# Spreading four pieces of token sums over two merges and the row blocks between them

## The chip, the cores and the metric

The kernel runs on one core of one Trainium2 chip. The metric is the time of one execution in device microseconds (us), and less is better. A core has five engines that run side by side, each with an instruction queue of its own that it works off in order: PE (matrix multiply, TensorE), ACT (ScalarE), DVE (VectorE), POOL (GpSimd) and SP (SyncE, which here only starts DMA transfers). An engine that waits for a semaphore holds everything that stands behind that instruction in its queue. On-chip data lie in SBUF, results of matmuls in PSUM; the DMA engines move data between these and the device's main memory (HBM).

## What is computed

The reference is one transformer-like block on 2048 tokens of width 1024, in float32. Cut to what matters here:

```python
merged = gate_a * (y_attn @ w_branch_attn) + gate_b * (y_gmlp @ w_branch_gmlp)
y = merged @ w_out
x = x + rmsnorm(y, norm_post_mix)
h = rmsnorm(x, norm_pre_mlp)
a = relu(h @ w_mlp_in)
x = x + rmsnorm((a * a) @ w_mlp_out, norm_post_mlp)
```

The parts before (input projections, dilated attention, chunked gMLP) are done when the stages of this document begin. The gates are sigmoids of stored projections.

## The kernel before

Tokens are worked in four chunks of 512, in the order 2, 3, 0, 1 (list `chunks`, line 986). This text calls them first to fourth chunk by that order, so the third is `c == 0` and the fourth `c == 1`. For each chunk there are two stages.

**Merge** (`merge`, line 885): eight slices `dt` of 128 output channels. For each slice PE makes the two branch products into PSUM (18 matmuls, names `b`, `yt`, `wb`). Two gates come from memory (`load_gate`, line 870, an SP transfer, line 873) into buffers `g` of which there are three for one branch and two for the other; ACT applies the sigmoid (`open_gate`, line 882); DVE multiplies gate and product (line 899) and adds the two (line 901); then `split` (ACT at line 70, DVE at line 78) makes a high and a low part of the result, called `mg`. Every matmul of this kernel is three matmuls of such parts (`mm3`, lines 95 to 97). The gates of a slice are asked for one slice ahead; those of the first two slices of the next chunk, and the next `yt`, are loaded after the first row block of this chunk.

**Row blocks** (`out_block`, line 912): four blocks of 128 tokens. SP loads the residual rows (`xr`, line 917, one buffer); PE multiplies `mg` with `w_out` (name `o`, 48 matmuls); ACT squares and sums (line 936), DVE scales (937), the residual is added (DVE, line 941), ACT sums its squares (943), POOL starts the store of `x1d` (944), and DVE writes the normed rows `y` (946). A second part of the block, run later by `flush` or `flush_older`, has PE transpose `y` (line 951, name `pt`), ACT copies it into `tt` (952), POOL starts two stores to `h2d` (953). `flush_older` runs in the middle of a later row block, when two blocks are open, and `flush` behind slices 0 and 2 of the next merge.

**Token sums** (`sums_t`, line 966). The MLP's first matmul is done by a scheme with fewer products, which needs sums and differences of quarters of `h2d`. For each half of the tokens there are four pieces, `k` from 0 to 3. A piece loads four tiles of 128 x 512 from `h2d` (SP, line 974), makes four subtractions on POOL (lines 975 to 978) and starts four stores to `t_d` on POOL (line 980). Two of the four tiles lie in one buffer `tq` (one copy, `bufs=1`), the other two in `tr` (two copies); both belong to the pool `ttp`, which the fourth chunk's second row block gives back (`e2r.close()`). The trace shows all of them under the name `tq`, the stores under `td`. The sums of the half stored first (chunks 2 and 3) are made by `merge_sums` (line 982) in the third merge, one piece behind each of the slices 4, 5, 6 and 7. They are read as `T_first` at the start of the MLP, behind the fourth chunk.

**Order of the work.** The order on PE is that of the program. On the other engines a planner orders the instructions by the program's order and its estimate of when each can run, so an instruction may stand earlier than written. `behind()` (line 170) limits that: what is emitted inside it stands, on each of ACT, DVE, POOL and SP, behind the instruction that was emitted last on that engine. The sums of the other half, later in the kernel, use it already (lines 1346 to 1348).

```python
    def merge_sums(dt):
        if dt > 3:
            sums_t(1, dt - 4, ttp, "tq", "tr", 2)
```

Of the kernel before, what the change touches and what calls it, by code (L numbers as in the profile page):

```python
# [41 lines left out]
def block_kernel(ctx, tc, a, out):  # L42
# [4 lines left out]
    def stack(es, name, bufs=1, side=None, space=None):  # L47
        kw = dict(name=name, bufs=bufs, reuse_waits="tile")
        if side:
            kw["side"] = side  # L50
        if space is not None:
            kw["space"] = space
        return es.enter_context(tc.tile_pool(**kw))
# [7 lines left out]
    def psum_mm(name):  # L61
        return ps.tile([P, 512], F32, name=name, tag="mm")
# [4 lines left out]
    def split(hi, lo, src, hi_eng="act", lo_eng="dve"):  # L67

        if hi_eng == "act":
            act.activation(hi, src, AF.Copy)  # L70
        elif hi_eng == "pool":
            pool.tensor_scalar(hi, src, 1.0, 1.0, op0=OP.mult, op1=OP.mult)  # L72
        else:
            dve.tensor_copy(hi, src)
        if behind_product is not None and lo_eng == "dve":
            behind_product.append((lo, src, f32(hi)))
        else:
            (pool if lo_eng == "pool" else dve).tensor_sub(lo, src, f32(hi))  # L78
# [15 lines left out]
    def mm3(ps, lh, ll, rh, rl, start, stop):  # L94
        pe.matmul(ps, lh, rh, start=start, stop=False)  # L95
        pe.matmul(ps, lh, rl, start=False, stop=False)  # L96
        pe.matmul(ps, ll, rh, start=False, stop=stop)  # L97
# [72 lines left out]
    def behind():  # L170

        es, t = ExitStack(), mybir.EngineType
        for e in (t.Activation, t.DVE, t.Pool, t.SP):
            es.enter_context(tc.issue_after(next(i for i in reversed(nc.cur_bb.bb.instructions) if i.engine == e)))
        return es
# [594 lines left out]
    for n in range(len(units) + 1):  # L770
        u = None
        if n < len(units):
            g, c, j = units[n]
# [73 lines left out]
    def load_y(c, engs=("act", "dve")):  # L847
        cs = slice(c * 512, (c + 1) * 512)
        yt = [bot.tile([P, 2, 512], F32R, name=f"yt{c}{k}", tag=f"yt{k}") for k in range(6)]
        for k in range(6):  # L850
            split_in(yt[k], ya_d[k, :, cs] if k < 2 else yg_d[k - 2, :, cs], None, *engs)
        return yt
# [17 lines left out]
    def load_gate(c, dt, wch):  # L870
        if (c, dt, wch) not in gates:
            gt = gtp.tile([P, 512], F32, name=f"g{wch}_{c}{dt}", tag=f"gt{wch}", bufs=3 - wch)
            sp.dma_start(gt, gate_d[wch * 8 + dt, :, c * 512:(c + 1) * 512])
            gates[c, dt, wch] = gt
# [3 lines left out]
    def open_gate(c, dt, wch):  # L878
        if (c, dt, wch) not in opened:
            load_gate(c, dt, wch)  # L880
            gt = gates[c, dt, wch]
            act.activation(gt, gt, AF.Sigmoid)
            opened.add((c, dt, wch))

    def merge(c, yt, between, each=None):
        cs = slice(c * 512, (c + 1) * 512)
        mg = []
        for dt in range(KT):
            dsl = slice(dt * P, (dt + 1) * P)
            if dt % 4 == 0:  # L890
                mg.append(mgp[dt // 4].tile([P, 2, 4, 512], F32R, name=f"mg{c}{dt}", tag="mg"))
            parts = []
            for wch, ks in ((0, range(0, 2)), (1, range(2, 6))):
                open_gate(c, dt, wch)
                gt = gates.pop((c, dt, wch))
                p = psum_mm(f"b{wch}_{c}{dt}")
                for k in ks:
                    mm3(p, wb[k][:, 0, dsl], wb[k][:, 1, dsl], yt[k][:, 0, :], yt[k][:, 1, :], k == ks[0], k == ks[-1])
                dve.tensor_mul(gt, gt, p)
                parts.append(gt)  # L900
            dve.tensor_add(parts[0], parts[0], parts[1])
            split(mg[-1][:, 0, dt % 4, :], mg[-1][:, 1, dt % 4, :], parts[0])
            if dt < KT - 1:
                for wch in range(2):
                    open_gate(c, dt + 1, wch)
            if each:
                each(dt)
            if dt in between:
                between[dt]()
        return mg  # L910
# [55 lines left out]
    def sums_t(half, k, pl, tag, tag2, bufs2):  # L966

        w = pl.tile([P, 2, 512], F32, name=f"tq{half}{k}", tag=tag, bufs=1)
        b11, b12 = w[:, 0], w[:, 1]
        b21, b22 = ((wp3 if pl is not ttp else pl).tile([P, 512], F32, name=f"tq{half}{k}{n}", tag=tag2, bufs=bufs2)  # L970
                    for n in range(2))
        t0 = half * HALF
        for t, kk, c in ((b11, k, 0), (b12, k, 1), (b22, k + 4, 1), (b21, k + 4, 0)):
            sp.dma_start(t, h2_d[:, kk, t0 + c * 512:t0 + c * 512 + 512])
        pool.tensor_sub(b11, b12, b11)
        pool.tensor_sub(b12, b22, b12)
        pool.tensor_sub(b22, b22, b11)
        pool.tensor_sub(b21, b21, b22)
        for name, t in (("T1", b11), ("T3", b12), ("T2", b22), ("T4", b21)):
            pool.dma_start(t_d[half][:, T_AT.index(name), k], t)  # L980

    def merge_sums(dt):
        if dt > 3:
            sums_t(1, dt - 4, ttp, "tq", "tr", 2)

    chunks = (2, 3, 0, 1)
    FIRST = ((0, 0), (1, 0), (0, 1), (2, 0), (1, 1))
# [14 lines left out]
    def load_b(half, name):  # L1002

        w = r3.tile([P, 2, 4, 512], F32R, name=f"{name}_{half}", tag=name, bufs=1)
        for k in range(0, 4, 2):
            t0, k0 = half * HALF, k + (4 if name == "B21" else 0)
            split_in(w[:, :, k:k + 2], h2_d[:, k0:k0 + 2, t0:t0 + 512], None, "act")
        b_[half, name] = w
# [39 lines left out]
    def lone_a(half, q, n, raw=None):  # L1048
        raw_lone(half, q, n, raw)
        split_lone(half, q, n)  # L1050
# [147 lines left out]
    ttp = None  # L1198
    yt = load_y(2, ("pool", "pool"))
    early_gates(2)  # L1200
    mg = merge(2, yt, {}, spatial_out)
    for n, c in enumerate(chunks):
        if n:
            mg = merge(c, yt, {0: flush, 2: flush}, merge_sums if c == 0 else None)
        for i in range(4):
            b = out_block(c, i, mg, flush_older)
            next(b)
            last.append(b)
            if n < 3 and not i:
                yt = load_y(chunks[n + 1])  # L1210
                for dt in range(2):
                    for wch in range(2):
                        load_gate(chunks[n + 1], dt, wch)
            if n == 3 and i == 1:
                e2r.close()
                rx = stack(e3, "rx", 1, side="right")
                spare = rx.tile([P, 512], F32, name="ar1_4", tag="xs", bufs=LEAD + 1)
                r3 = stack(er, "r3", 1, side="right")
                for name in ("B11", "B21"):
                    load_b(1, name)  # L1220
                for o, (q, n_) in enumerate(FIRST):
                    raw = gtp.tile([P, 512], F32, name=f"ar{n_}_{q}", tag=f"gt{o % 2}", bufs=3 - o % 2)
                    lone_a(1, q, n_, raw.rearrange("p (k c) -> p k c", k=4))
# [111 lines left out]
    tq = stack(eq, "tq", 1)  # L1335
# [440 lines left out]
```

## Time and profile before

| what | value |
|---|---|
| median of 3 runs | 2699.76 us (2698.89 to 2700.78) |
| the profiled execution | 2700.86 us |
| its span | 2698.8 us |
| mean granted clock of PE | 0.996 of full speed |
| busy share PE, DVE, ACT, POOL | 99%, 59%, 39%, 36% |
| packets of SP's DMA queue q1 | 43.5% of 16 engines' span |

The span is the time from the first to the last instruction that the profiler recorded on the core; the profiled execution's time also holds what lies around it, 2.06 us. A line of the timeline reads: start, duration, engine, line of the code, operation, output `<-` inputs by the program's names, count, and in brackets the idle time of the engine just before it with what ended that idle time. SPq, PEld and the like are the engine's queue or its weight loads. A table by windows gives, for each stretch of time, the busy time of every engine in it and the clock that was granted to PE.

### The profile page before, as it was taken

To read this page: it belongs to the slowest core of one execution; us is meant where nothing else is said; L and a number is where in the kernel's file an instruction comes from. 1 tells how busy PE (TensorE), PEld (TensorE's weight loads), DVE (VectorE), ACT (ScalarE), POOL (GpSimd) and SP (SyncE) were. 2 spreads that over 40 slices of the span, in tenths; PEclk is the share of its full clock that TensorE was granted. 3 is DMA by queue.
4 is the path that set the end of the run, shared out by engine and by line. 5 is a ranking of instruction groups with operands and counts; after the bars stand their busy time and mean duration, and the time that the engine had idled before them with its cause. 6 is when DMAs were issued, how large, how long until landed. Compare 5 with 4: busy or idle time off the path is not lost. (4 is left out here: it accounts for less than half of the span.)

```text
span 2698.8 us, 34839 instructions
## 1 busy us (share of the span) xinstructions
PE 2663.4 (99%) x12674; PEld 2226.9 (83%) x12674; DVE 1582.5 (59%) x2677; ACT 1053.2 (39%) x2149; POOL 977.2 (36%) x837
## 2 busy tenths in 40 slices
PE   9999999999999999999899999999999999999998
PEld 8888888888888888888678888888888888888887
DVE  5665463334444345665456765555437888888866
ACT  5213111144444432344335555565545333333334
POOL 0351352210050004210413454323224776676645
PEclk9999999999999999999999999999999999999999
DMA  7445446266577846654656465554344212222236
GB/s 271 167 144 180 152 141 218 96 189 199 177 248 205 220 151 187 202 177 145 227 172 251 133 207 178 173 183 125 114 136 129 84 57 86 88 86 87 92 108 212
DMA packets 299197, 431.77 MB, mean 160 GB/s; under 512 B 52817, under 2 KB 166225, under 8 KB 299026
## 3 DMA queue, kind: packets, MB, share of 16 engines
q1 hardware_dynamic: 226864, 370.48, 43.5%
q10 hardware_dynamic: 64178, 32.06, 3.9%
q0 software_dynamic: 7984, 27.01, 2.6%
q8 instruction: 100, 1.64, 0.3%
q14 instruction: 71, 0.58, 0.1%
HBM read 286.67 MB, written 142.80 MB: 159 GB/s over the span
## 5 line engine op out<-in xcount | busy, mean ns | idle before, releaser
L1627 PE MATMUL ya<-T_spots,s 128*128 128x512 f32 x1176 | 289.4, 390 | 0.7 <-ACT T_spots L70 0.6
L1627 PEld LDWEIGHTS ya<-T_spots,s 128*128 128x128 f32 x1176 | 220.6, 188 | 47.4 <-ACT T_spots L70 1.0
L70 ACT ACTIVATE s<-sraw 128x768 fp32r<-128x768 f32 (+1 forms) x184 | 127.2, 696 | 330.4 <-POOL sraw L1428 155.7
L78 DVE TENSOR_TENSOR s<-sraw,s 128x512 fp32r<-128x512 f32 x172 | 184.1, 1095 | 8.6 <-ACT s L70 8.5
L1104 PE MATMUL aa<-B,A 128*128 128x512 f32 x768 | 182.3, 390 | 0.7 <-DVE A L85 0.7
L1104 PEld LDWEIGHTS aa<-B,A 128*128 128x128 f32 x768 | 143.9, 188 | 31.2 <-DVE A L85 1.1
L1627 PE MATMUL yc<-T_spots,s 128*128 128x512 f32 x624 | 159.7, 389 | 0.0
L72 POOL TENSOR_SCALAR w_g<-w_g_r 128x1024 fp32r<-128x1024 f32 x32 | 34.1, 1080 | 344.5 <-PE g L97 258.0
L1075 POOL TENSOR_TENSOR s<-w1r 128x512 f32<-128x512 f32 x32 | 42.3, 1322 | 309.3 <-DVE S L78 256.6
L95 PE MATMUL x<-hT_a,wq 128*128 128x512 f32 x384 | 149.8, 390 | 0.0
L96 PE MATMUL x<-hT_a,wq 128*128 128x512 f32 x384 | 149.5, 389 | 0.0
L97 PE MATMUL x<-hT_a,wq 128*128 128x512 f32 x384 | 149.5, 389 | 0.0
L709 DVE TENSOR_REDUCE o<-po 128x256 f32<-128x512 f32 x48 | 33.1, 690 | 184.3 <-PE po L708 184.3
L1627 PEld LDWEIGHTS yc<-T_spots,s 128*128 128x128 f32 x624 | 117.2, 188 | 24.3
L70 ACT ACTIVATE hl<-r 128x512 fp32r<-128x512 f32 x48 | 30.4, 632 | 238.1 <-POOL r L307 89.0
L95 PE MATMUL o<-wo,mg 128*128 128x512 f32 x256 | 102.1, 399 | 8.1 <-ACT mg L70 7.5
L78 POOL TENSOR_TENSOR T_spots<-w2r,T_spots 128x512 fp32r<-128x512 f32 x70 | 104.5, 1522 | 7.3 <-ACT T_spots L70 7.3
L95 PE MATMUL g<-hT_b,w_g 128*128 128x512 f32 x256 | 104.7, 409 | 0.0
L95 PE MATMUL g<-hT_a,w_g 128*128 128x512 f32 x256 | 104.3, 407 | 0.0
L78 DVE TENSOR_TENSOR A<-w1r,A 128x512 fp32r<-128x512 f32 x61 | 61.8, 1014 | 66.9 <-ACT A L70 66.9
L96 PE MATMUL o<-wo,mg 128*128 128x512 f32 x256 | 101.0, 394 | 0.0
L97 PE MATMUL o<-wo,mg 128*128 128x512 f32 x256 | 100.9, 394 | 0.0
(390 smaller groups left out, 7156.2 us busy)
## 6 DMA issues: line engine op xcount, KB each, us to landing
w1r<-in_w_mlp_in_dram SPq DMA_DIRECT2D x64, 512.0 KB, 3.8
sraw<-sd SPq DMA_DIRECT2D x128, 256.0 KB, 3.3
qk<-hl SPq DMA_DIRECT2D x24, 1024.0 KB, 5.1
qq<-qk SPq DMA_DIRECT2D x96, 256.0 KB, 4.9
w_g_r<-in_w_in_dram SPq DMA_DIRECT2D x32, 512.0 KB, 5.5
gated<-gt SPq DMA_DIRECT2D x64, 256.0 KB, 3.5
w2r<-in_w_mlp_out_dram SPq DMA_DIRECT2D x16, 1024.0 KB, 6.4
sd<-u ACTq DMA_DIRECT2D x63, 256.0 KB, 3.8
```

What stands on the lines that cost most here:

```text
L70: act.activation(hi, src, AF.Copy)
L72: pool.tensor_scalar(hi, src, 1.0, 1.0, op0=OP.mult, op1=OP.mult)
L78: (pool if lo_eng == "pool" else dve).tensor_sub(lo, src, f32(hi))
L95: pe.matmul(ps, lh, rh, start=start, stop=False)
L96: pe.matmul(ps, lh, rl, start=False, stop=False)
L97: pe.matmul(ps, ll, rh, start=False, stop=stop)
L709: dve.tensor_reduce(ot[:, :, j * 64:(j + 1) * 64], po.rearrange("p (b h e) -> p b e h", b=4, h=2), axis=AX.X, op=OP.add)
L1075: pool.tensor_add(s1, a21, a22)
L1104: pe.matmul(p, w[:, l, k, :], h[:, r, k, :], start=i in (1, 6, 5) and not k and not n, stop=k == 3 and n == 2, skip_group_check=True)
L1627: pe.matmul(p, s[:, l], w[r], start=i in (1, 2, 5) and not m and not o, stop=m == 1 and o == 2, skip_group_check=True)
```

## The change

The pieces of the half stored first stand at other places. Piece 0 comes behind slice 3 of the third merge, pieces 1 and 2 behind the second and the fourth row block of the third chunk, piece 3 behind slice 3 of the last merge. Each is emitted inside `behind()`. What a piece does is the same.

```diff
     def merge_sums(dt):
-        if dt > 3:
-            sums_t(1, dt - 4, ttp, "tq", "tr", 2)
+        if dt == 3:
+            sums_ahead(0)
+
+    def merge_sums_last(dt):
+        if dt == 3:
+            sums_ahead(3)
+
+    def sums_ahead(k):
+        with behind():
+            sums_t(1, k, ttp, "tq", "tr", 2)
...
     for n, c in enumerate(chunks):
         if n:
-            mg = merge(c, yt, {0: flush, 2: flush}, merge_sums if c == 0 else None)
+            mg = merge(c, yt, {0: flush, 2: flush}, merge_sums if c == 0 else merge_sums_last if c == 1 else None)
         for i in range(4):
             b = out_block(c, i, mg, flush_older)
             next(b)
             last.append(b)
+            if n == 2 and i % 2:
+                sums_ahead(1 + i // 2)
```

## The prediction

> **What bounds the kernel now.** I read the page first: span and busy time. The profiled execution took 2700.86 us, 2.06 us more than its span.
>
> ```profile
> span 2698.8 us, 34839 instructions
> PE 2663.4 (99%) x12674; PEld 2226.9 (83%) x12674; DVE 1582.5 (59%) x2677; ACT 1053.2 (39%) x2149; POOL 977.2 (36%) x837
> ```
>
> PE, the matrix engine, is busy in all but 35.4 us. The change removes no matmul and adds none, so it can only act on the time in which PE stands still or runs on a slow clock. Next I read the timeline of PE alone for the first matmul of each merge (output `b`) and of each stage of row blocks (output `o`), and the table by windows cut there. Two of those boundaries, as the timeline shows them:
>
> ```profile
> 1308.86 0.39 PE L95 MATMUL o<-wo,mg 128*128 128x512 f32 x1
> ...
> 1369.72 0.39 PE L95 MATMUL b<-yt,wb 128*128 128x512 f32 x1
> ```
>
> The table; its columns are window, length and PE busy, then PEld, DVE, ACT and POOL busy, PE clock, DMA share and GB/s:
>
> ```profile
> 1194.70:1229.13 34.43, 34.43 (x161) 28.70 (x160) 22.79 (x42) 15.10 (x27) 3.55 (x5) 1.00 0.54 157
> 1229.13:1274.44 45.31, 45.31 (x210) 37.72 (x209) 23.60 (x56) 20.97 (x45) 4.66 (x7) 1.00 0.45 154
> 1274.44:1308.86 34.42, 34.42 (x161) 28.69 (x160) 22.31 (x41) 14.47 (x26) 11.39 (x13) 1.00 0.58 183
> 1308.86:1369.72 60.86, 49.83 (x209) 40.68 (x208) 25.19 (x55) 20.81 (x45) 25.72 (x29) 0.89 0.61 208
> 1369.72:1406.89 37.17, 35.21 (x161) 28.39 (x160) 23.31 (x45) 15.57 (x30) 5.06 (x7) 1.00 0.56 168
> 1406.89:1452.20 45.31, 45.31 (x210) 37.70 (x209) 28.99 (x61) 22.06 (x44) 4.67 (x7) 1.00 0.49 170
> ```
>
> Rows 1, 3 and 5 are the second, third and last merge; 2, 4 and 6 the row blocks behind them. Equal PE work takes 34.42 and 45.31 us where nothing stops it. The third chunk's row blocks take 60.86, **15.55 us more**; the last merge 37.17, **2.75 us more**. Together 18.30 us is all that these stages can give. The stops inside, from the timeline of PE (in brackets: idle time before the instruction and what ended it):
>
> ```profile
> 1320.59 0.79 PE L95 MATMUL o<-wo,mg 128*128 128x512 f32 x1 [7.49 <-ACT mg L70]
> ...
> 1322.04 0.63 PE L95 MATMUL o<-wo,mg 128*128 128x512 f32 x1
> ...
> 1349.04 1.94 PE L951 MATMUL pt<-ident,y 128*128 128x128 f32 x8 [3.55 <-DVE y L946]
> ...
> 1398.77 0.50 PE L95 MATMUL b<-yt,wb 128*128 128x512 f32 x1 [1.06 <-DVE g L899]
> ...
> 1404.04 0.50 PE L95 MATMUL b<-yt,wb 128*128 128x512 f32 x1 [0.89 <-DVE g L899]
> ```
>
> Two stops, 7.49 and 3.55, make 11.04 of the 15.55. The other 4.5 is clock: the granted clock is 0.89 in that window, and a matmul behind the first stop takes 0.63 instead of 0.39. I put half of it, about 2.2, on each. The last two stops make 1.95 of the 2.75.
>
> **Who causes the first stop.** The timeline of SP and ACT around it, and from the view of waits of SP its longest one:
>
> ```profile
> 1306.60 4.65 SPq L974 DMA_DIRECT2D tq<-h2d  x4
> ...
> 1311.34 1.95 SPq L873 DMA_DIRECT2D g<-gated  x3
> ...
> 1317.32 0.63 ACT L882 ACTIVATE g<-g 128x512 f32<-128x512 f32 x1 [10.05 <-DMA g<-gated]
> ...
> 1319.93 0.61 ACT L70 ACTIVATE mg<-g 128x512 fp32r<-128x512 f32 x1
> ```
>
> ```profile
> SPq L974 <- DMA td<-tq: 15.1, 4, 7.1
> ```
>
> Read upwards: PE waits for `mg`; ACT made it late because its queue stood 10.05 us at a sigmoid whose gate had not arrived; that gate was issued at 1311.34, behind four loads of the second piece of token sums. SP held them for the stores of the first piece, since `tq` has one buffer. The four pieces (I number them 0 to 3, as the code's `k`) stand one behind the other, and every gate behind them waits too.
>
> **And the second.** Next on SP came the third piece, ahead of the rest of `yt`:
>
> ```profile
> 1322.41 1.75 SPq L974 DMA_DIRECT2D tq<-h2d  x4
> ...
> 1331.52 1.97 ACT L70 ACTIVATE yt<-yt 128x512 fp32r<-128x512 f32 x3 [7.19 <-DMA yt<-ygd]
> ...
> 1341.37 2.83 DVE L941 SCALAR_TENSOR_TENSOR xr<-y,r_post,xr 128x1024 f32<-128x1024 f32 x1
> ...
> 1347.61 1.28 DVE L946 SCALAR_TENSOR_TENSOR y<-xr,r_pm,gmlp 128x1024 f32<-128x1024 f32 x1
> ```
>
> ACT stands 7.19 us at `yt`, so the first block's norm starts late; DVE's L941 then takes 2.83 beside POOL's fourth piece, and L946 gives `y` just before PE moves on at 1349.04. The late chain of these blocks also runs into the last merge; I take its 2.75 as the same lateness, because the second merge, equal in shape and without it, has no stop.
>
> **The change, part by part.** The work of a piece is the same: four loads on SP, four subtractions and four DMA issues on POOL. From first to last instruction on POOL, and the landing of the stores (view of line 980):
>
> ```profile
> 1311.72 1.28 POOL L975 TENSOR_TENSOR tq<-tq 128x512 f32<-128x512 f32 x1 [4.65 <-DMA tq<-h2d]
> ...
> 1318.25 1.10 POOL L980 DMA_DIRECT2D td<-tq  x2
> ```
>
> ```profile
> DMA to landing us min/median/max: 2.3/2.8/7.4
> ```
>
> That is 7.63 us on POOL. A piece holds `tq` from its loads to its landed stores: 1306.60 to 1322.41, 15.81 us between two sets of loads.
>
> *Where the pieces will stand.* The second chunk's stages show the undisturbed pattern; the third chunk follows 79.74 us later (1274.44 less 1194.70). POOL, SP, DVE and PE rows that place them:
>
> ```profile
> 1250.60 20.30 SPq L917 DMA_DIRECT2D xr<-in_x_dram  x3
> ...
> 1285.13 7.69 SPq L873 DMA_DIRECT2D g<-gated  x4
> ...
> 1295.29 2.83 SPq L974 DMA_DIRECT2D tq<-h2d  x3
> ...
> 1298.23 3.29 SPq L873 DMA_DIRECT2D g<-gated  x3
> ```
>
> ```profile
> 1255.42 0.55 POOL L944 DMA_DIRECT2D x1d<-xr  x1 [8.57 <-DVE xr L941]
> ...
> 1267.14 0.55 POOL L944 DMA_DIRECT2D x1d<-xr  x1 [7.49 <-DVE xr L941]
> ...
> 1279.11 0.55 POOL L944 DMA_DIRECT2D x1d<-xr  x1 [7.72 <-DVE xr L941]
> 1280.89 0.75 POOL L953 DMA_DIRECT2D h2d<-tt  x1 [1.23 <-ACT r_pm L102]
> ```
>
> Piece 0 keeps its place: its loads wait for the `h2d` stores of the flush before it and come at 1295.29. Piece 1 goes on SP behind the load of `xr` of the second block, 1250.60 + 79.74 = 1330.3; piece 2 behind that of the fourth, 20 us later, 1350.3; piece 3 behind the gates of the fifth slice in the last merge, within 1285.13 to 1292.82 plus 79.74, so about 1371. The distances are 35, 20 and 20 us, all over 15.81: no load should find `tq` taken. **The first stop goes (7.49 and its clock), and the second (3.55 and its clock), and with the late chain the last merge's 2.75.**
>
> *What it costs, piece 0.* SP still holds the gates behind it, from 1292.82 to 1298.23, 5.4 us. In the trace of before the same hold stands in the third merge, and that window is all busy. If no slack were left by the last slices, a part of it would reach PE: between 0 and 3 us, the nearest row (34.42 busy of 34.42) at 0; I take 0.5.
>
> *Pieces 1 and 2 on POOL.* Behind the store of `x1d` of the second block, 1255.42 + 0.55 + 79.74 = 1335.7, POOL works until 1343.3. What queues behind it is the store of `h2d` for the first block, which nobody awaits before `tt` comes round two blocks later, and the next `x1d` store at 1267.14 + 79.74 = 1346.9, which frees `xr`: 3.6 us of room. Piece 2 starts at 1359.4, in the last merge, and ends at 1367.0, or 1368.5 with two `h2d` issues of 0.75 between.
>
> DVE's slack against PE in these blocks, from rows of the second chunk:
>
> ```profile
> 1257.50 1.28 DVE L946 SCALAR_TENSOR_TENSOR y<-xr,r_pm,gmlp 128x1024 f32<-128x1024 f32 x1
> ...
> 1268.11 0.38 PE L951 MATMUL pt<-ident,y 128*128 128x128 f32 x2
> ```
>
> `y` is ready 9.3 us before PE transposes it. L941 took 2.83 beside POOL against L946's 1.28, so a collision costs 1.55 and is hidden here.
>
> The Trainium skill has a rule that speaks against putting pieces between row blocks: "SBUF — State Buffer", section "Who interferes with whom", says that a vector instruction with two SBUF inputs and a GpSimd instruction that reads SBUF exclude each other, the later one standing still until the other is done. The 2.83 agrees with it. By that rule the collisions become a rival, priced from rows below.
>
> *Pieces 2 and 3 in the last merge.* Four issues on SP, 1.75 us, stand ahead of a gate; a collision may add 1.55. Without slack that is 3.3 us on PE, with the slack of the third merge 0. I take 1.0.
>
> **Sum.** 2700.86 - 15.55 - 2.75 + 0.5 + 1.0 = 2684.1 for the profiled execution. The median of the runs, 2699.76, lies 1.10 under it, so the forecast is **2683.0**.
>
> **The rivals.**
>
> B. *The hold returns in the last merge.* Piece 2's last stores are issued on POOL by 1367.0 to 1368.5 and land 2.8 later, at 1369.8 to 1371.3; piece 3's loads come at about 1371. With a landing of 7.4 SP waits some 4 us, and the gates of the last slices with it. For it: no margin. Against: third-merge slack took 5.4. Full price that of the first stop, 7.49 + 2.2 = 9.7: 2692.7.
>
> C. *DVE held up.* Twelve subtractions move beside DVE's norms; if each cost 1.55 on the path, 18.6 us come back: 2681.5 + 18.6 = 2700.1. Against it: the 9.3 us of slack and DVE busy 23.60 of 45.31. The rule of the Trainium skill in "SBUF — State Buffer" stands behind this rival.
>
> D. *Not done as said.* The edit gives only the earliest place of pieces 1 and 2; the planner may still push both into the last merge. There three pieces stand in a row and the old stops come back one stage later: about 2699.8. Against it: their inputs and buffers are ready long before.
>
> E. *Slower.* One mechanism: SP's queue in order, with one `tq`. If a piece needs longer than the 20 us between places (15.81 now; it decides when the excess is over the slack), each of the three moved pieces holds SP in front of an `xr` load or a gate, and each makes a stop of 9.7: 2681.5 + 29.1 = 2710.6.
>
> **How the numbers follow.** Chances: forecast 0.76, B 0.11, C 0.04, D 0.05, E 0.04. The floor is 2699.76 - 18.30 = 2681.5, less 0.9 for the spread of the runs: 2680.5. Both costs at their upper ends (3 and 3.3) give 2681.5 + 6.3 = 2687.8; a partial hold of B carries it to 2690. I leave out full B, C, D and E. Of this kernel 0.2%, 5.4 us, is about what a measurement can tell from no change: faster is below 2694.4, the forecast and B, 0.87; same C and D, 0.09; slower E, 0.04.
>
> **What would show it.** Right: row blocks of the third chunk back near 45.31 us at clock 1.00, the last merge near 34.42, loads of pieces 1 to 3 with no wait for `td`, no idle of PE before a transpose of `pt`. Wrong: a wait of L974 for `td` in the last merge and a sigmoid standing behind it (B); L941 or L946 at 2.8 with PE waiting for `y` (C); two sets of `tq` loads less than 16 us apart (D, E). The forecast fails if the last merge keeps its 2.75 without the late chain: then 2684 to 2686.

## The result: faster, by half of what was forecast

The changed kernel takes 2690.60 us (median of 7 runs, 2688.11 to 2696.89), the kernel before beside it 2699.74 (7 runs, 2696.95 to 2701.33). The ratio is 0.9970, with a 95% interval from 0.9958 to 0.9981. So the change gains 9.1 us, more than the 0.2% that a measurement can tell from nothing, and not the 16.7 of the forecast; the time lies 0.6 us above the upper end of the range.

### The profile page after: what moved, and what is told of

Read it like the earlier page. It is cut to its first block, busy times and chain, and to the rows that moved or that the text cites. A ratio compares the mean times of both kernels' runs of the same rounds, so it can differ in the third digit from the quotient of the medians.

```text
span 2688.7 us, 34842 instructions
## 1 busy us (share of the span) xinstructions
PE 2660.5 (99%) x12674; PEld 2225.8 (83%) x12674; DVE 1586.6 (59%) x2677; ACT 1052.1 (39%) x2149; POOL 975.7 (36%) x837
## 5 line engine op out<-in xcount | busy, mean ns | idle before, releaser
L95 PE MATMUL o<-wo,mg 128*128 128x512 f32 x256 | 101.3, 396 | 3.4 <-DVE g L899 2.4
L70 ACT ACTIVATE S<-w1r 128x512 fp32r<-128x512 f32 x96 | 60.1, 629 | 106.3 <-PE ac L1112 63.9
L97 PE MATMUL o<-wo,mg 128*128 128x512 f32 x256 | 100.6, 393 | 0.0
```

## The profile after

The profiled execution of the changed kernel took 2690.6 us. Span and busy time from its page:

```profile
span 2688.7 us, 34842 instructions
PE 2660.5 (99%) x12674; PEld 2225.8 (83%) x12674; DVE 1586.6 (59%) x2677; ACT 1052.1 (39%) x2149; POOL 975.7 (36%) x837
```

PE does the same work in a span that is 10.1 us shorter. The table by windows, cut at the first matmul of each stage: second merge, third merge, row blocks of the third chunk, last merge (columns as in the table before):

```profile
1196.11:1230.54 34.43, 34.43 (x162) 28.70 (x160) 21.50 (x41) 14.52 (x27) 3.55 (x5) 1.00 0.50 143
...
1276.84:1313.06 36.22, 34.72 (x162) 28.63 (x160) 23.37 (x41) 14.46 (x26) 11.05 (x13) 1.00 0.60 188
1313.06:1359.51 46.45, 45.88 (x209) 37.52 (x208) 27.52 (x58) 21.52 (x46) 12.09 (x15) 1.00 0.53 182
1359.51:1395.65 36.14, 35.02 (x161) 28.54 (x160) 25.87 (x41) 14.46 (x26) 19.24 (x22) 1.00 0.86 276
```

The row blocks fall from 60.86 to 46.45, at full clock. But the third merge, 34.43 with four pieces before, now takes 36.22 with one, and the last merge only falls from 37.17 to 36.14. Over these three stages the gain is -14.41 + 1.79 - 1.03 = -13.65. The other 3.5 us of the difference of 10.1 lie in stages that the edit does not touch (the first merge is 1.66 longer, its row blocks 1.53). In the profiles of this study such stages vary by themselves: the first merge from 42.57 to 46.49. Differences of one to two microseconds between single profiles are not read as an effect below.

The stops of PE in these stages, from its timeline:

```profile
1310.21 0.50 PE L95 MATMUL b<-yt,wb 128*128 128x512 f32 x1 [1.50 <-DVE g L899]
...
1317.87 0.50 PE L95 MATMUL o<-wo,mg 128*128 128x512 f32 x1 [0.57 <-ACT mg L70]
...
1382.70 0.50 PE L95 MATMUL b<-yt,wb 128*128 128x512 f32 x1 [0.84 <-DVE g L899]
...
1392.80 0.50 PE L95 MATMUL b<-yt,wb 128*128 128x512 f32 x1 [0.28 <-DVE g L899]
```

The stops of 7.49 and 3.55 are gone. What is new is a stop of 1.50 in the third merge. SP's side, first its timeline (the piece loads and what stands around them), then its waits:

```profile
1299.33 1.61 SPq L974 DMA_DIRECT2D tq<-h2d  x3
1301.04 11.58 SPq L873 DMA_DIRECT2D g<-gated  x6
...
1338.16 1.74 SPq L974 DMA_DIRECT2D tq<-h2d  x4
...
1359.40 1.83 SPq L974 DMA_DIRECT2D tq<-h2d  x4
...
1377.37 2.35 SPq L974 DMA_DIRECT2D tq<-h2d  x4
1382.07 11.74 SPq L873 DMA_DIRECT2D g<-gated  x6
```

```profile
SPq L974 <- DMA h2d<-tt: 4.3, 2, 3.9
...
SPq L974 <- DMA td<-tq: 0.6, 1, 0.6
```

The pieces stand 39, 21 and 18 us apart, and hardly wait for stores any more (0.6, where before it was 22.4 in the same stretch; the 15.1 of the prediction's view ends before the fourth piece). But piece 0 still holds SP for 3.9 us, for the `h2d` stores of the flush, with six gates behind it.

## The experiments

**Theory.** In the kernel before, four pieces come one behind each slice, every 4.3 us (34.43 by 8), where one takes POOL 7.63. They hold up what shares queues with them, and spreading ends that. **Rivals** on the same gain: the single buffer `tq` alone holds SP; SP's queue alone; POOL's queue. **Open after the result** is where the other 7 to 8 us went: collisions of POOL's subtractions with DVE, the hold of SP in front of gates, late landing of gates beside the piece transfers, or a floor that was never there.

All were timed beside the kernel before. Stages are in us on PE from first matmul to first matmul, from one profiled execution each; the ratio has its 95% interval. Two profiles of one kernel (changed and e1) differ by 0.65 in the third merge, by 0.99 in the row blocks and by 2.21 in the last merge.

| kernel | median us | ratio to before | third merge | row blocks | last merge |
|---|---|---|---|---|---|
| before | 2699.74 | | 34.43 | 60.86 | 37.17 |
| changed | 2690.60 | 0.9970 (0.9958 to 0.9981) | 36.22 | 46.45 | 36.14 |
| e1 changed again | 2689.81 | 0.9967 (0.9954 to 0.9979) | 36.87 | 47.44 | 38.35 |
| e2 no subtractions | 2688.53 | 0.9953 (0.9940 to 0.9965) | 35.94 | 45.83 | 35.29 |
| e3 piece 0 written in the row blocks | 2690.17 | 0.9962 (0.9949 to 0.9974) | 34.45 | 46.43 | 39.31 |
| e4 before, loads by POOL | 2703.39 | 1.0013 (1.0004 to 1.0022) | 34.86 | 62.95 | 36.95 |
| e5 changed, loads by POOL | 2693.25 | 0.9979 (0.9970 to 0.9988) | 35.34 | 50.60 | 38.12 |
| e6 piece 3 written behind the merge | 2697.87 | 0.9992 (0.9983 to 1.0001) | 37.19 | 46.43 | 38.17 |
| e7 all pieces written in row blocks | 2698.38 | 0.9997 (0.9988 to 1.0006) | 35.29 | 46.48 | 43.09 |
| e8 no pieces | 2683.03 | 0.9940 (0.9928 to 0.9953) | 34.42 | 45.99 | 34.79 |
| e9 before, two buffers | 2698.64 | 0.9995 (0.9986 to 1.0004) | 36.21 | 57.25 | 35.71 |
| e10 changed, two buffers | 2691.79 | 0.9966 (0.9954 to 0.9979) | 36.30 | 47.59 | 36.25 |
| e11 piece 2 a block earlier | 2688.83 | 0.9958 (0.9946 to 0.9971) | 35.16 | 47.73 | 36.24 |
| e12 piece 0 two slices later | 2687.93 | 0.9951 (0.9939 to 0.9964) | 34.43 | 47.09 | 38.53 |
| e13 changed, gates two ahead | 2689.29 | 0.9966 (0.9954 to 0.9979) | 36.70 | 47.06 | 38.50 |
| e14 before, gates two ahead | 2695.69 | 0.9987 (0.9979 to 0.9996) | 36.11 | 56.98 | 35.72 |
| e15 e11 and e12 joined | 2686.42 | 0.9952 (0.9939 to 0.9966) | 34.43 | 46.85 | 39.72 |
| e16 e12 with gates two ahead | 2690.84 | 0.9965 (0.9952 to 0.9977) | 34.43 | 46.64 | 39.17 |
| e17 e12, no subtractions | 2688.00 | 0.9957 (0.9943 to 0.9970) | 34.88 | 49.37 | 38.62 |
| e18 e12, subtractions by DVE | 2685.84 | 0.9953 (0.9940 to 0.9965) | 34.48 | 46.01 | 36.75 |

### What the pieces cost in all: e1 and e8

e1 is the changed kernel, once more. e8 leaves the four pieces out, and the MLP reads unsummed tiles in their place.

```diff
     def sums_ahead(k):
-        with behind():
-            sums_t(1, k, ttp, "tq", "tr", 2)
+        pass
```

> The changed kernel once more, unaltered. Theory (the shortfall against the forecast has a local part of about 4.8 us, caused by the moved pieces in the two merges and the row blocks, and the rest is spread between runs in stages whose order of work did not change): third merge, row blocks and last merge again near 36.2, 46.5 and 36.1 us, while the first merge, the first row blocks and the MLP differ from the first profile by up to 2 us either way. Rival (the change made other stages slower too): those other stages repeat their excess over the kernel before, 1.7 us in the first merge, 1.5 us in the first row blocks and 1.0 us in the MLP's first matmul.

> The pieces of the half stored first are left out, and the MLP reads unsummed tiles in their place, so the first matmul of that half is not computed rightly. It measures the floor of these stages. Forecast's view (undisturbed stages take 34.4, 45.3 and 34.4 us): third merge, row blocks and last merge at these lengths, time 2681 to 2682.5. Rival (the shortest length seen is not the usual one, since gates that land late stop PE for 0.4 to 1 us in most merges): sum of the three stages 1 to 3 us over 114.2, time 2683 to 2686.

The table by windows of e8: third merge, row blocks, last merge.

```profile
1276.04:1310.46 34.42, 34.42 (x161) 28.68 (x160) 21.67 (x41) 14.89 (x27) 3.56 (x5) 1.00 0.49 146
1310.46:1356.45 45.99, 45.88 (x209) 37.53 (x208) 24.46 (x58) 20.86 (x45) 4.68 (x7) 1.00 0.46 154
1356.45:1391.24 34.79, 34.72 (x161) 28.60 (x160) 21.39 (x41) 14.61 (x27) 3.56 (x5) 1.00 0.49 142
```

Without pieces the three stages take 115.20 us, and the kernel 2683.03: that is the floor, and the forecast was as low as this floor. In the kernel before the pieces cost 2699.12 - 2683.03 = 16.1 us (medians of kernels timed together), in the changed one some 7: 2690.60 or 2689.81, less 2683.03 (timed apart, each beside a kernel before of 2699.12 to 2700.27). Compared with e8, the last merge of the changed kernel has 0.86 of the DMA engines busy in place of 0.49, and DVE busy 25.87 in place of 21.39 with the same 41 instructions.

### Who made the stops of before: e4, e9, e14

e4: the loads of the pieces are started by POOL, so that SP's queue never holds a gate for them; the places are those of before.

```diff
-            sp.dma_start(t, h2_d[:, kk, t0 + c * 512:t0 + c * 512 + 512])
+            (pool if half else sp).dma_start(t, h2_d[:, kk, t0 + c * 512:t0 + c * 512 + 512])
```

> The kernel before, with all four pieces in the third merge as they were, but the loads of the pieces started by POOL instead of SP, so that no gate stands behind them in SP's queue. Theory of the forecast (the stops came from SP's queue held for the one tq buffer): no stop of 7.5 us at the first row block, row blocks of the third chunk near 46 to 50 us instead of 60.9, some 8 to 14 us less than the kernel before. Rival (four pieces in a row are too much for POOL and DVE at that place, whoever starts the loads): row blocks stay above 56 us and the time near the kernel before.

PE's stops and POOL's queue in e4:

```profile
1318.45 0.79 PE L95 MATMUL o<-wo,mg 128*128 128x512 f32 x1 [4.96 <-ACT mg L70]
...
1364.49 1.94 PE L951 MATMUL pt<-ident,y 128*128 128x128 f32 x8 [7.42 <-ACT junk L936]
```

```profile
1351.59 1.09 POOL L980 DMA_DIRECT2D td<-tq  x2
1352.68 0.55 POOL L944 DMA_DIRECT2D x1d<-xr  x1
```

The first stop shrinks from 7.49 to 4.96 and does not go, so SP's queue is only a part of it. What is left in e4 is a gate that lands late: SP issued it at 1308.9, it landed 8.2 us later, and ACT stood at it for 3.35:

```profile
1317.25 0.63 ACT L882 ACTIVATE g<-g 128x512 f32<-128x512 f32 x1 [3.35 <-DMA g<-gated]
```

The second stop grows from 3.55 to 7.42: on POOL the first `x1d` store has no idle in front of it, it comes right behind the fourth piece, and frees `xr` that much later. The kernel is no faster, rather slower (1.0004 to 1.0022).

e9: the places of before, with two copies of `tq` and three of `tr`.

```diff
-        w = pl.tile([P, 2, 512], F32, name=f"tq{half}{k}", tag=tag, bufs=1)
+        w = pl.tile([P, 2, 512], F32, name=f"tq{half}{k}", tag=tag, bufs=2 if half else 1)
...
-            sums_t(1, dt - 4, ttp, "tq", "tr", 2)
+            sums_t(1, dt - 4, ttp, "tq", "tr", 3)
```

> The kernel before with two copies of `tq` and three of `tr` for the half stored first; places of the pieces as before. Theory (the four pieces stand too close for one buffer, so that SP is held for the stores of the piece before, and POOL is strung out behind SP): SP's longest wait of L974 for td falls from 7.1 to under 3 us, the first stop of PE (7.49) falls under 3, POOL is done with the four pieces some 10 us earlier, the third chunk's row blocks take 46 to 51 us, time 2686 to 2692, so most of what the spread gains without any moved piece. Rival 1 (POOL's queue of four pieces in front of the x1d store, whoever feeds it): the first stop goes, the second stays or grows, row blocks 54 to 63, time 2693 to 2703. Rival 2 (DMA bandwidth of four pieces in a row delays the gates): both stops stay, 58 to 62, time within 2 us of before.

SP's wait for stores in e9, and PE's stops:

```profile
SPq L974 <- DMA td<-tq: 10.3, 7, 4.1
```

```profile
1319.42 0.80 PE L95 MATMUL o<-wo,mg 128*128 128x512 f32 x1 [4.72 <-ACT mg L70]
...
1349.54 1.06 PE L951 MATMUL pt<-ident,y 128*128 128x128 f32 x8 [2.50 <-DVE y L946]
```

One buffer does string the pieces out: with two copies POOL is done with the fourth at 1334.8 in place of 1348.2, SP's wait for stores falls from 22.4 to 10.3, and both stops shrink. But the third merge grows by 1.79, and the time is that of before, so the theory that the one buffer makes the cost falls. The pieces come faster than POOL can do them, so the next loads only wait one piece later, in front of the gates: the gate at the first stop was issued at 1313.41, behind loads that had waited 4.1, and ACT stood at it for 5.96:

```profile
1313.41 0.40 SPq L873 DMA_DIRECT2D g<-gated  x1
...
1318.22 0.63 ACT L882 ACTIVATE g<-g 128x512 f32<-128x512 f32 x1 [5.96 <-DMA g<-gated]
```

The gates that are asked for around the first row block also land late. From issue to landing of the gates (line 873) between 1310 and 1355 us, for before, e9, and the changed kernel:

```profile
DMA to landing us min/median/max: 5.9/7.9/8.9
```

```profile
DMA to landing us min/median/max: 7.9/8.3/8.5
```

```profile
DMA to landing us min/median/max: 3.2/4.7/6.8
```

Beside four pieces in a row the median is some 8 us, in the changed kernel 4.7, and without pieces (e8, the same stretch) 4.2. But most of these are gates of the next merge, issued behind the first stop: in the kernel before those four took 7.9 to 8.9, and the three in front of the stop 5.9 to 6.4. So the first stop is a gate that SP issues late (before, e9) or that lands late (e4, and in part before). Of the rival of transfer traffic the time came true in e9, the stops did not stay. The rival of POOL's queue falls here, since POOL stood idle 10.33 us in front of that `x1d` store:

```profile
1345.16 0.54 POOL L944 DMA_DIRECT2D x1d<-xr  x1 [10.33 <-DVE xr L941]
```

e14: before, with gates asked for two slices ahead (one more buffer for the second gate).

```diff
+                if c != 2 and dt < KT - 2:
+                    for wch in range(2):
+                        load_gate(c, dt + 2, wch)
```

> The kernel before with gates asked for two slices ahead in the same way. Theory (its first stop is a late gate behind four pieces): the first stop of 7.49 falls by up to the 4.3 us of a slice, the second stop and the last merge stay, time 2693 to 2698. Rival (the gates two slices ahead stand behind the pieces too, since the buffers come free no earlier): time within 2 us of before.

The first stop falls to 3.34, and the time by 0.13% (0.9979 to 0.9996). So the stop is indeed a late gate, but the row blocks still take 56.98. Two halves of one cause, held queues and long landings, remain as long as the four pieces stand together. Spreading takes away both, which neither of the remedies for one of them did.

### Which places of the change matter: e3, e5, e6, e7

```diff
# e3: pieces 0, 1 behind row blocks 1, 2 of the third chunk, 2 behind the fourth
-            mg = merge(c, yt, {0: flush, 2: flush}, merge_sums if c == 0 else merge_sums_last if c == 1 else None)
+            mg = merge(c, yt, {0: flush, 2: flush}, merge_sums_last if c == 1 else None)
...
-            if n == 2 and i % 2:
-                sums_ahead(1 + i // 2)
+            if n == 2 and i != 2:
+                sums_ahead(min(i, 2))
# e6: piece 3 behind the fourth chunk's first row block
+            if n == 2 and i % 2 or n == 3 and not i:
+                sums_ahead(1 + i // 2 if n == 2 else 3)
# e7: pieces 0, 1, 2 behind row blocks 1, 2, 3, and piece 3 as in e6
+            if n == 2 and i < 3 or n == 3 and not i:
+                sums_ahead(i if n == 2 else 3)
```

e5 is the changed kernel with the edit of e4.

> Piece 0 comes behind the first row block of the third chunk in place of the third merge; pieces 1, 2 and 3 as in the changed kernel. Both the theory (subtractions beside DVE) and its rival (the hold on SP) expect the third merge at 34.4 to 34.9 us, 1.3 to 1.8 us less. They differ in the row blocks: the theory expects them at 46 to 48 us, since DVE has room there; if a piece in front of an xr load or beside the norms matters, they rise to 50 us or more and the gain is lost.

> The changed kernel with the loads of its pieces started by POOL instead of SP, so that no gate and no xr load stands behind them in SP's queue; the subtractions stay. Theory A (what is left in the third merge is the hold of gates behind piece 0 on SP): third merge 34.4 to 35.0 us against 36.2 and 36.9 in two profiles of the changed kernel. Theory B (it is the subtractions beside DVE): third merge still 35.5 to 37 us. Row blocks 46 to 48 us by both, as POOL's wait for a landing comes ahead of an x1d store only once.

> The changed kernel with piece 3 moved out of the last merge, behind the fourth chunk's first row block. If piece 3 costs the last merge its excess (36.1 and 38.4 us in two profiles against 34.4), that merge comes to 34.4 to 35.5 us and the time falls by 1 to 3 us. Rival (the excess of the last merge is the late chain of the third chunk's blocks and piece 2): the last merge stays at 36 to 38 us.

> No piece in a merge: pieces 0, 1 and 2 behind the first three row blocks of the third chunk, piece 3 behind the first of the fourth. Places are 11.8 us apart, under the 15.8 us that a piece held its buffer in the kernel before, so SP waits for the stores in front of xr loads. If the collisions and holds in the merges are what is left, both merges come to 34.4 to 35 us and the time to 2684 to 2687. Rival (the distance decides): row blocks rise above 50 us and the time lies above that of the changed kernel.

These edits moved less than was meant. The load of `xr` stands early in SP's queue, and the loads of a piece that is written behind its row block stand soon after it, so piece 0's loads are still in the third merge in e3 and e7, and piece 3's in the last merge in e6 and e7. Only subtractions and stores moved. SP in e3 (its third merge runs from 1274.24 to 1308.69) and in e6 (last merge from 1357.81 to 1395.97):

```profile
1285.35 0.38 SPq L974 DMA_DIRECT2D tq<-h2d  x1
...
1295.58 2.45 SPq L974 DMA_DIRECT2D tq<-h2d  x3
```

```profile
1373.17 0.32 SPq L974 DMA_DIRECT2D tq<-h2d  x1
...
1374.74 3.25 SPq L974 DMA_DIRECT2D tq<-h2d  x3
```

The third merge of e3 takes 34.45 although these loads waited 3.6 in it for the flush's stores. The time is found again in the last merge (39.31): the same time, moved. e5 is no faster than the changed kernel and probably slower (the intervals overlap), with a stop of 3.35 at the first row block. Its third merge, 35.34, lies between the two theories. Its last merge takes 38.12 with no piece's load on SP, so a hold of SP by such loads is not what that excess needs. In e6 and e7 the MLP starts late; PE at its first matmul in e6:

```profile
1450.83 2.72 PE L1112 MATMUL aa<-B,A 128*128 128x512 f32 x6 [3.07 <-ACT xs L1126]
```

The MLP's first stage takes 621.3 and 621.4 us there, against 614.9 to 615.9 in before, the changed kernel, e1 and e8. There POOL comes to piece 3 only at 1412.48, behind the `x1d` store of the fourth chunk's first row block, and SP's loads of `B` for the MLP, which waited for the piece's stores, come at 1420.56 (1400.44 in the changed kernel). Which way the 6 us arise is not shown, but the subtractions and stores of piece 3 are better off in the last merge. Without them that merge still takes 38.17 in e6, so they alone do not make its excess.

### Where the other 7 us are: e2, e10, e11, e12, e13, e15 to e18

e2: the changed kernel without the four subtractions of a piece.

> The changed kernel with the four subtractions of each of the four pieces left out: the loaded tiles are stored as they are, so the sums, and with them the MLP's first matmul for half of the tokens, are not computed rightly. Loads on SP and stores on POOL stay. Theory (POOL's subtractions hold up DVE's instructions with two inputs in SBUF, seen as 2.30 instead of 0.69 us for a low part of mg): third merge back to 34.4 to 34.9 us, last merge to 34.4 to 35.0 us, together some 3 us less. Rival (SP holds the gates behind the loads of a piece, subtractions do not matter): both merges stay at about 36.2 and 36.1 us.

The median is 1 to 2 us lower, which the overlapping intervals do not settle, and the third merge stays at 35.94. The collisions that they make are in the trace of the changed kernel, on DVE in the third merge:

```profile
1301.74 0.69 DVE L78 TENSOR_TENSOR mg<-g,mg 128x512 fp32r<-128x512 f32 x1 [4.33 <-ACT mg L70]
...
1307.26 2.30 DVE L78 TENSOR_TENSOR mg<-g,mg 128x512 fp32r<-128x512 f32 x1 [2.52 <-ACT mg L70]
```

The same instruction takes 0.69 alone and 2.30 beside POOL. (This agrees with the rule of the Trainium skill, "SBUF — State Buffer", section "Who interferes with whom".) In time they are a small part. They do show in the third merge. In nine profiles of the changed kernel and its variants piece 0's loads wait in this merge for the flush's stores: in five of them (changed, e1, e6, e10, e13) one such instruction takes 1.89 to 2.30 and the merge 36.22 to 37.19, in the other four (e2, e3, e7, e11) all take 0.69 at most and the merge 34.45 to 35.94.

e10: two buffers as in e9, in the changed kernel. e11: piece 2 behind the third row block. e12: piece 0 behind slice 5 of the third merge.

```diff
# e11
-            if n == 2 and i % 2:
-                sums_ahead(1 + i // 2)
+            if n == 2 and i in (1, 2):
+                sums_ahead(i)
# e12
     def merge_sums(dt):
-        if dt == 3:
+        if dt == 5:
             sums_ahead(0)
```

> The changed kernel with two copies of `tq` and three of `tr`. Its loads of pieces 1 to 3 hardly wait for td (longest 0.6 us), so both theories expect no change: 2689 to 2691. Were it 2 us or more faster, the one buffer would still cost something in the changed kernel by a way that the waits do not show.

> The changed kernel with piece 2 behind the third row block of the third chunk in place of the fourth. Theory (piece 2's work on POOL and its loads beside the first slices of the last merge make that merge's excess of 1.4 to 3.6 us over the kernel without pieces): last merge 34.8 to 35.5, row blocks 46 to 48, time 2687 to 2690. Rival (the excess comes of gates that are asked for late, whichever piece it is): last merge stays at 36 to 39, or gets longer as it did with all pieces in the row blocks (43.09), time 2690 to 2696.

> The changed kernel with piece 0 behind slice 5 of the third merge in place of slice 3: its loads no longer stand waiting for the flush's h2d stores (3.9 us in the changed kernel). Theory (that hold on SP makes the third merge's 1.5 to 2.4 us): third merge 34.4 to 35.0, rest as before, time 2688 to 2690. Rival (the piece's four issues in front of the gates, not the wait, do it, or the last gates have no slack): third merge 35.5 or more, or a stop of 1 us or more at the first row block for `mg`; time 2690 to 2693.

e10 shows no effect of the buffer, as expected. e11 leaves the last merge at 36.24. Three of piece 2's four subtractions still stand in it (from 1359.18 on), so this says little about piece 2. e12 does what the theory of the hold said: by then the flush's stores have landed. Its SP timeline (no wait of line 974 for `h2d` is left):

```profile
1287.16 11.26 SPq L873 DMA_DIRECT2D g<-gated  x6
1298.52 1.83 SPq L974 DMA_DIRECT2D tq<-h2d  x4
```

The third merge is 34.43 there, and 34.43 to 34.88 in e15, e16, e17 and e18, which share the edit; in the nine profiles named above it is 34.45 to 37.19. So the move takes the excess away. How much of it is the hold, and how much the slowed DVE instruction that goes with it, is open: e3 has the hold and 34.45, e2 the hold without any subtraction and 35.94. The last merge does not shrink with the move.

e13 and e16: gates two ahead, in the changed kernel and in e12. e15: e11 and e12 joined.

> The changed kernel with a third copy of the second gate buffer, and with the gates of a slice asked for two slices ahead in place of one in the last three merges. Theory (the pieces' remaining cost is that gates come late to merges that run at the pace of their gates): third merge 34.4 to 35.0 and last merge 34.4 to 35.2, rows 46 to 47, time 2685 to 2688. Rival (the cost is DVE's collisions and queue order, not the gates): both merges keep 35.5 to 38, time 2689 to 2691.

> The changed kernel with piece 0 behind slice 5 of the third merge and piece 2 behind the third row block, both moves that ran alone at 2687.9 and 2688.8. If their gains add up: 2686 to 2687.5. If each only moves the same lateness from one stage to the next: 2688 to 2691, with the last merge at 36 to 39.

> Piece 0 behind slice 5 and the gates two slices ahead. Theory of the late gates: at least as good as the gates alone, both merges under 35.2, time 2684 to 2687, within 4 us of the kernel without pieces (2683.0). Rival: the last merge keeps 36 to 38.5, time 2687 to 2690.

Both merges of e13 keep their excess, as does the last merge of e16. But in e13 the gates are not asked for earlier: SP issues those of the third merge 5.7, 10.7, 18.8 and 24.7 us behind its start (in e1 5.7, 10.7, 18.7 and 24.9), since it waits there for DVE to free a buffer (14.4 us in all, 14.3 in e1). So the theory that an earlier request takes the late gates away is not tested by e13. e15's time lies where gains that add up would put it, while its profile has 39.72 in the last merge, as the rival said; that profiled execution, 2692.7, was the longest of its five, and the median tells more.

e17: e12 without subtractions. e18: e12 with the subtractions on DVE, two slices or a row block behind their loads, and so no subtraction on POOL.

```diff
# e18, in sums_t for the half stored first
-        pool.tensor_sub(b11, b12, b11)
...
+        def rest(eng):
+            eng.tensor_sub(b11, b12, b11)
...
+    def sums_rest():
+        with behind():
+            rest_.pop(0)(dve)
```

> Piece 0 two slices later, and the subtractions left out (the loaded tiles are stored as they are). Theory (hold in the third merge and collisions behind it make nearly all of the cost): third merge 34.4, row blocks 45.5 to 46.2, last merge 34.6 to 35.4, time 2683.5 to 2686, within 3 us of the kernel without pieces (2683.0). Rival (the traffic of the pieces delays gates, 0.75 to 0.83 of the DMA engines busy in the last merge against 0.50): last merge keeps 36 to 38.5, time 2686 to 2689.

> Piece 0 two slices later, and the subtractions made by DVE, two slices or a row block behind the loads of their piece, so that no subtraction of POOL meets DVE. All sums are computed. Theory (collisions): DVE has 16 instructions of 0.69 more, 11 us, and is busy 20 to 26 of 36 us in the last merge, so it hides most of them: last merge 34.6 to 36, time 2684 to 2687. Rival (traffic, or DVE's own added work takes the place of the collisions): last merge 36.5 or more, or new stops for mg; time 2687 to 2692.

The theory that hold and collisions make nearly all of the cost falls with e17: with no subtraction of these pieces its median is that of e12, and its last merge takes 38.62 (in the longest of its five executions; in e2, also without, it took 35.29). SP, ACT and PE there, and the gates' way from issue to landing in this stage:

```profile
1377.94 1.79 SPq L974 DMA_DIRECT2D tq<-h2d  x4
1379.82 14.55 SPq L873 DMA_DIRECT2D g<-gated  x6
```

```profile
1387.91 1.22 ACT L882 ACTIVATE g<-g 128x512 f32<-128x512 f32 x2 [4.06 <-DMA g<-gated]
```

```profile
1393.36 0.50 PE L95 MATMUL b<-yt,wb 128*128 128x512 f32 x1 [2.33 <-DVE g L899]
```

```profile
DMA to landing us min/median/max: 3.3/6.1/8.0
```

The gates behind piece 3's four loads land late, ACT waits 4.06 for one, and PE stops for the product made from it. Without pieces (e8) the median from issue to landing in the last merge is 3.7, in the changed kernel 4.6. In e18 the same gates come late as well, on ACT:

```profile
1383.17 0.63 ACT L882 ACTIVATE g<-g 128x512 f32<-128x512 f32 x1 [3.74 <-DMA g<-gated]
```

Its time is what the theory of collisions gave, its last merge, 36.75, is the rival's. So the last merge's excess needs neither the arithmetic on POOL (e17, e18) nor loads on SP (e5). That it comes of the gates' landing is not shown either: the median there is 5.3 in e2 with a last merge of 35.29, and 4.3 in e12 with 38.53. What makes this excess stays open.

**A better version.** e18, e15 and e12 compute every sum and have ratios of 0.9953, 0.9952 and 0.9951, against 0.9970 and 0.9967 of the changed kernel. They beat the kernel before, each by its interval. Against the changed kernel the intervals overlap, and e16, with the same move, has 0.9965; that they are 2 to 5 us faster than it is likely, and not settled.

## Why the prediction was right in sign and wrong in size

1. *PE bounds the kernel, only its stops can go.* Right: same matmuls, shorter span.
2. *Both stops go with their clock.* Right: neither is left, the row blocks run at 1.00.
3. *The first stop is SP, held for one `tq`.* Half right. SP was held, and the wait for `td` fell from 22.4 to 0.6. But with the loads off SP (e4) 4.96 of the stop remain, behind a gate that took 8.2 us to land, and with two buffers (e9) 4.72, behind a gate that SP still issued late. The forecast needed only that the spread removes it, which holds by either way.
4. *The places: loads 35, 20 and 20 us apart, none finds `tq` taken.* Right: 39, 21 and 18. So rivals B, D and E did not come: no hold for `td` returned, the pieces stand as written.
5. *Cost of piece 0: "I take 0.5".* Too small: the third merge grew by 1.79 and 2.44 in two profiles, inside the stated 0 to 3. The row taken, a merge all busy with the same hold, was no sign of how much slack the gates have. Moving piece 0 two slices on (e12) takes the excess away, and with it both the hold and a DVE instruction slowed to 2.30. Which of the two carries how much is open.
6. ***"Pieces 2 and 3 in the last merge … I take 1.0."*** **This is the step that failed**, with step 5: against 34.42 the last merge is 1.7 and 3.9 us longer in two profiles of the changed kernel, up to 5.3 in the other kernels that have piece 3 at this place (e15). I priced four issues on SP (1.75) and one collision (1.55), and counted on slack for most of that. The runs show that this price was too low by 0.7 to 2.9, and not by which way: the excess stays without piece loads on SP (e5, 38.12) and without subtractions (e17, 38.62, in its longest execution), and it does not follow the landing time of the gates (e2 and e12). My own condition of failure, the last merge keeping its 2.75 without the late chain, is what came; the time that I gave for it, 2684 to 2686, was too low since the other terms missed too.
7. *The floor.* 2681.5 forecast, 2683.03 measured (e8): row blocks take 45.99 without any piece, and most profiles lose some time at their start (PE waits 0.57 for `mg` there in the changed kernel). 45.31 was the best case and was taken for the usual one. That the forecast, 2683.0, equals the measured floor is chance.
8. *Rival C, collisions on the path.* They exist (2.30 for 0.69) but cost at most some 2 us (e2, and nothing that can be told in e17 against e12), not 18.6.

In numbers: forecast 2681.5 + 1.5; measured 2683.0 + 7.6. Of the miss 1.5 is the floor, 6.1 the price of the moved pieces. That the pieces cost some 7 us is shown by e8; of their way to PE in the last merge only what it does not need is known.

## What to carry to other kernels

A stage that is fully busy shows that its feeds were in time, not that they have slack, so the issue time of a moved transfer is no safe price for it there. Look in the trace for where a moved task stands: an edit that names one place for all of it can move the arithmetic and leave the loads (e3, e6, e7). Before adding buffers or changing the queue, compare the rate at which a task is asked for with the rate at which its engine does it; where it was asked for too often, more buffers (e9) and another queue (e4) did not help, and spacing did. And measure the kernel without the task early: the floor bounds the gain better than a sum of stops.

## What the runs showed of the hardware

The length of PE's stop does not tell whether the clock falls behind it. The table by windows for some 9.5 us behind a stop of 3.34 (e14), of 3.49 (e17), of 2.37 (the changed kernel, first chunk's row blocks) and of 3.55 (before); the clock is the third number from the end, the DMA share behind it:

```profile
1316.70:1326.00 9.30, 8.43 (x26) 6.33 (x27) 5.68 (x7) 2.22 (x5) 4.24 (x6) 0.69 0.71 224
```

```profile
1317.40:1327.00 9.60, 9.51 (x41) 7.58 (x42) 6.28 (x11) 7.26 (x15) 0.00 (x0) 1.00 0.47 145
```

```profile
1149.00:1159.00 10.00, 9.95 (x37) 8.05 (x38) 8.95 (x14) 6.30 (x11) 0.00 (x0) 0.83 1.00 373
```

```profile
1349.00:1359.00 10.00, 9.96 (x37) 8.44 (x38) 2.69 (x8) 1.01 (x2) 0.19 (x1) 0.73 0.36 133
```

The shortest of the four lost clock and the second longest did not, and the DMA share does not sort them either; what decides stays open. The Trainium skill, "TensorE: Matmul & The Clock Gate", section "HAM oscillation — how this bites in real kernels", warns of idle gaps above about 3.4 us. The stop of 2.37 that lost clock and that of 3.49 that lost none differ from it, and here the measurement decides.

The other surprise is the gates' landing: around the third chunk's first row block a transfer of 256 KB took a median of 4.2 us with no piece about (e8), and 7.9 (before) and 8.3 (e9) beside four.
